# Gating the side matmuls of a one-layer hybrid decoder to every fourth step, moving delta-net arithmetic from GpSimd to VectorE, and spreading the small inverse products

## The chip, the cores and the metric

The kernel runs on one core of a Trainium2 chip. A core has five engines with instruction queues of their own: TensorE (PE, the matmuls; its weight loads are listed as PEld), VectorE (DVE), ScalarE (ACT), GpSimd (POOL) and SyncE (SP, which here issues all the DMAs). Matmul results land in PSUM, everything else lies in SBUF. The metric is the device time of one execution in microseconds (us), the median of several runs; lower is better.

## The reference, cut to what matters

One decoder layer with `D_MODEL` 2048 over 16 learned meta tokens and 256 real tokens (272 positions in all), float32:

```
u = rmsnorm(h, attn_norm_w); proj = u @ w_in          # 2048 x 7184
o_a = diff_attention(aq, ak, av, ...)                 # 8 heads, two softmax maps a head
o_d = gated_deltanet(dq, dk, dv, dz, db, da, ...)     # 8 heads, chunked delta rule
h = h + concat([o_a, o_d]) @ w_out
u = rmsnorm(h, ffn_norm_w)
h = h + (silu(u @ w_gate) * (u @ w_up)) @ w_down      # hidden 5632
```

In the delta net q, k and v pass a causal convolution of four taps and SiLU, q and k are normalised, and each chunk needs the decay matrix `exp(gc_i - gc_j)` below the diagonal, the product `k k^T` scaled with it, the inverse of the unit lower triangular matrix `1 + L` made of it, and the state that goes from chunk to chunk:

```
decay = where(incl, exp(diff), 0)
lmat = where(strict, einsum(kb, kc) * decay, 0)
u, w = solve(1 + lmat, ...)
qk = einsum(qc, kc) * decay
v_new = u_c - w_c @ S;  o = (q_c * exp(g_c)) @ S + qk_c @ v_new
S = S * exp(g_last) + (k_c * exp(g_last - g_c))^T @ v_new
o = rmsnorm(o, o_norm_w) * silu(z)
```

## The kernel before, in words

**Main stream.** Every large product is made of three passes in a reduced float32 type: each weight tile `raw` (512 KB, loaded by SP into a ring of `WR` = 4) is split into `hi` (ACT copy, L250) and `lo` (DVE subtraction, L251), both in rings of `WS` = 4, and the activations are split in the same way. `proj` (L1086) multiplies 28 groups of 256 columns of `w_in`: first k, v, q and z of the delta net, then k, q and v of the attention, two heads at a time. A weight tile of `proj` carries 24 matmuls. `stream` (L1133) does the output projection, the gate, up and down projections.

**Side tasks.** Everything else is written as Python generators, run by `Tasks`. After each k-tile `proj` calls `tasks.step()` (six matmuls of the main stream per step), and `stream` calls it twice per k-tile. A step resumes up to `PER_STEP` = 2 tasks in list order. A task that yields a number sleeps that many steps, one that yields a condition sleeps until it holds. A `Ring` counts the live buffers of a pool: `aux` has four PSUM banks, and a task that wants to put side matmuls on TensorE takes one with `yield from aux.get(...)` and releases it with `aux.free()` once the reading instruction has been written down. `r1` (12 buffers) and `r2` (10) hold SBUF scratch. The four PSUM banks of `mm` belong to the main stream.

**What sets the order.** `manual_schedule` pins ACT and SP to the order in which the code writes their instructions. The instructions of PE, DVE and POOL are put into queues by the framework's planner: program order is the priority, but an instruction which the planner holds to be not ready is overtaken. [...]

**The delta net.** `decay` makes the decay matrix of a unit (four heads of one 128-position block): POOL multiplies a mask with the gate column (L475), four side matmuls (L479), an exponential on ACT, and POOL applies the triangle (L485). There are four units and the meta block. `unit` then multiplies that by `c1` on POOL (L792), forms `k k^T` (L795), multiplies both on DVE (L798), and waits for the inverse. `inverses` writes the 128x128 matrices to DRAM and back in 16x16 pieces, inverts these in 15 steps on DVE (L630, L631), returns them through DRAM, and doubles the size twice with many small products: L663 (a group of 32x32 pieces), a copy to SBUF, L677, a subtraction, with sleeps of two, one and two steps between them. POOL makes its masked operand at L624. After the inverse `unit` runs a chain of PSUM groups (L808, L819, L828, L836, L844, L851, L861); its `ks` is scaled by POOL at L815. `meta_block` has POOL scale eight `ksm` slices (L759). `z_task` applies SiLU on ACT and the output norm weight on POOL (L911); the gated result is formed at L888.

**Start.** SP issues `aw`, then pieces of `xT` with weight tiles 0 to 3 between them, then `w_ba`, `cmask` and `par`. The loop over k-tiles splits the input into `xh` and `xl` (L325, L326) and splits weight tile 0 in two halves after k = 0, and tiles 1, 2, 3 whole after k = 5, 9 and 13.

## Time and profile before

| what | value |
|---|---|
| time, median of 3 runs | 1263.71 us (1262.24 to 1264.34) |
| the profiled execution | 1262.79 us |
| its span, first to last instruction | 1261.0 us |
| mean granted TensorE clock | 0.996 |
| DMA, mean over the span | 178 GB/s |

The profiled execution took 1.8 us more than its span; that is what lies around the first and last instruction. The page lists busy time by engine, the span in slices, the chain of work that ended last, and groups of instructions by source line. A matmul in float32 is recorded as two instructions. In a timeline a bracket such as `[3.07 <-DVE gT L735]` gives the idle time of the engine just before the row, and the instruction that ended it. In a windows table each row is a stretch of the span: busy us and number of instructions of PE, PEld, DVE, ACT and POOL, then the granted clock as a share of full speed, the DMA share and GB/s. In the chain each row has a start, a length in us, and what the time was spent on.

### The profile page before, as it was taken

Reading aid. Unit: us, or ns where it says so; the run is one execution under the profiler, and the core shown is the slowest. Engines: PE = TensorE matmul, PEld = TensorE weight load, DVE = VectorE, ACT = ScalarE, POOL = GpSimd, SP = SyncE. Lnnn points to the kernel's source line nnn. Section 1 sums busy time; section 2 is a strip of 40 time slices with the busy share of each in tenths; the row PEclk is TensorE's granted clock in tenths of the full one; section 3 lists DMA queues with packets and bytes.
Section 4 is the critical chain, followed back from the end, with each engine's and each line's share of the span. In section 5 each row is a group of like instructions: output and inputs, shape, how many; then the busy total and the mean of one; then the engine's idle time right before and its main releaser. Section 6 shows DMA issues by size and latency. Waiting matters only on the chain.

```text
span 1261.0 us, 18878 instructions
## 1 busy us (share of the span) xinstructions
PE 1244.4 (99%) x7469; PEld 1092.2 (87%) x7469; DVE 729.4 (58%) x1084; ACT 610.9 (48%) x962; POOL 46.8 (4%) x48
## 2 busy tenths in 40 slices
PE   8999999999999999999999999999999999999998
PEld 7998989999999988888888888888888888888886
DVE  7789956567676666645544554554455454544443
ACT  6664454466776655544344444444444433343332
POOL 0322200110000000000000000000000000000000
PEclk9999999999999999999999999999999999999999
DMA  8456642345544655566665566556666555656562
GB/s 270 134 168 176 179 138 85 118 151 167 158 144 151 218 167 183 177 194 191 190 190 190 187 192 192 184 186 198 185 189 194 187 191 190 215 189 213 191 210 83
DMA packets 150280, 224.31 MB, mean 178 GB/s; under 512 B 11560, under 2 KB 72368, under 8 KB 149936
## 3 DMA queue, kind: packets, MB, share of 16 engines
q1 hardware_dynamic: 150192, 223.11, 55.8%
q8 instruction: 58, 0.95, 0.3%
q14 instruction: 30, 0.25, 0.1%
HBM read 219.73 MB, written 3.35 MB: 177 GB/s over the span
## 4 chain that ended last, share of the span: by engine, by line
PE 89%; DVE 6%; ACT 2%; DMA 1%; issue 1%; SPq 0%; DVEq 0%; ACTq 0%
PE mm L1133 64%; PE mm L1086 19%; DVE lo L251 2%; DVE r L514 1%; DMA raw<-in_w_in_dram 1%; PE aux L1216 1%; PE aux L1034 1%; ACT hi L250 1%; PE aux L989 1%; DVE r L630 0%; PE aux L1021 0%; PE aux L381 0%; SPq L276 0%; DVE r L631 0%; DMA e<-r 0%
## 5 line engine op out<-in xcount | busy, mean ns | idle before, releaser
L251 DVE TENSOR_TENSOR lo<-raw,hi 128x1024 fp32r<-128x1024 f32 (+1 forms) x409 | 504.9, 1236 | 469.5 <-ACT hi L250 468.4
L250 ACT CAST hi<-raw 128x1024 fp32r<-128x1024 f32 (+1 forms) x409 | 428.8, 1050 | 546.7 <-PE mm L1133 447.7
L1133 PE MATMUL mm<-hi,uh 128*128 128x512 f32 x704 | 274.9, 390 | 0.0
L1133 PE MATMUL mm<-hi,ul 128*128 128x512 f32 x704 | 274.0, 389 | 0.0
L1133 PE MATMUL mm<-lo,uh 128*128 128x512 f32 x704 | 273.9, 389 | 0.0
L1086 PE MATMUL mm<-xh,hi 128*128 128x272 f32 (+2 forms) x896 | 260.7, 291 | 1.6 <-ACT hi L250 1.6
L1086 PE MATMUL mm<-xh,lo 128*128 128x272 f32 (+2 forms) x896 | 255.6, 286 | 3.0 <-issue 1.8
L1086 PE MATMUL mm<-xl,hi 128*128 128x272 f32 (+2 forms) x896 | 256.7, 287 | 0.0
L1133 PE MATMUL mm<-hi,hT 128*128 128x512 f32 x704 | 217.2, 389 | 0.0
L1086 PEld LDWEIGHTS mm<-xh,hi 128*128 128x128 f32 x896 | 169.6, 189 | 5.8 <-issue 3.0
L1086 PEld LDWEIGHTS mm<-xh,lo 128*128 128x128 f32 x896 | 168.8, 189 | 1.9 <-DVE lo L251 1.9
L1086 PEld LDWEIGHTS mm<-xl,hi 128*128 128x128 f32 x896 | 169.3, 189 | 0.3 <-DVE xl L326 0.2
L1133 PEld LDWEIGHTS mm<-hi,ul 128*128 128x128 f32 x704 | 132.1, 188 | 27.6
L1133 PEld LDWEIGHTS mm<-hi,hT 128*128 128x128 f32 x704 | 132.1, 188 | 27.3
L1133 PEld LDWEIGHTS mm<-hi,uh 128*128 128x128 f32 x704 | 132.2, 188 | 27.1
L1133 PEld LDWEIGHTS mm<-lo,uh 128*128 128x128 f32 x704 | 132.2, 188 | 27.0
L1133 PE MATMUL mm<-lo,hT 128*128 128x512 f32 x352 | 136.9, 389 | 0.0
L1133 PEld LDWEIGHTS mm<-lo,hT 128*128 128x128 f32 x352 | 66.1, 188 | 13.7
L514 DVE SCALAR_TENSOR_TENSOR r<-r,par_sb,r 128x272 f32<-128x272 f32 (+1 forms) x72 | 34.7, 541 | 0.2 <-ACT r L511 0.2
L1133 PE MATMUL mm<-hi,mix_d_hi 128*128 128x512 f32 x64 | 25.5, 399 | 0.0
L1133 PE MATMUL mm<-hi,mix_a_hi 128*128 128x512 f32 x64 | 25.1, 392 | 0.0
L1133 PE MATMUL mm<-hi,mix_d_lo 128*128 128x512 f32 x64 | 25.0, 390 | 0.0
(305 smaller groups left out, 849.8 us busy)
## 6 DMA issues: line engine op xcount, KB each, us to landing
raw<-in_w_in_dram SPq DMA_DIRECT2D x111, 512.0 KB, 3.6
raw<-in_w_gate_dram SPq DMA_DIRECT2D x88, 512.0 KB, 3.5
raw<-in_w_up_dram SPq DMA_DIRECT2D x88, 512.0 KB, 3.5
raw<-in_w_down_dram SPq DMA_DIRECT2D x88, 512.0 KB, 3.5
raw<-in_w_out_dram SPq DMA_DIRECT2D x32, 512.0 KB, 3.5
xr<-in_xT_dram SPq DMA_DIRECT2D x7, 272.0 KB, 6.0
x_k_c<-in_x_dram SPq DMA_DIRECT2D x1, 1024.0 KB, 6.5
x_q_c<-in_x_dram SPq DMA_DIRECT2D x1, 1024.0 KB
```

The lines of the kernel that those rows point to most:

```text
L250: S.copy(hi[:, js], raw[:, js])
L251: V.tensor_tensor(lo[:, js], raw[:, js], hi[:, js], ALU.subtract)
L514: V.scalar_tensor_tensor(acc, raw[:, off + j:off + j + m], cwv[:, ct, j:j + 1], acc, ALU.mult, ALU.add)
L989: PE.matmul(pss[m][:, cut[n]], q[ms, P * n:P * (n + 1)], k[ms, 0:NK[n]], start=True, stop=True)
L1034: PE.matmul(po[:, n, :], l, r, start=(j == 0), stop=(j == 1 + n))
L1086: PE.matmul(acc[c][:, 0:n], a[:, k, cs], b[:, kt, t0:T], start=(kt == 0 and i == 0), stop=(kt == KT - 1 and i == 2))
L1133: PE.matmul(acc[b], l, r[:, i % 2, :], start=(first and i == 0 and j == 0), stop=(last and i == len(kts) - 1 and j == 2))
L1216: PE.transpose(pst[:, j, :], g_[:, P * j:P * (j + 1)], ident)
```

## The change

There are four parts.

1. `aux.get` now also needs `tasks.slot()`, which holds in every fourth step (`SLOT` = 4). In such a step up to six tasks are resumed, in the others two as before. A side task that wants a PSUM bank therefore sleeps until the next slot; SBUF rings and the main stream's banks are not gated.
2. Delta-net arithmetic leaves POOL: the two products of `decay`, the masked operand of `inverses`, the `ksm` and `ks` scalings run on DVE. The multiplication by `c1` is no longer a step of its own but a factor in two DVE instructions, which become four instructions of 128x128 each. The output norm weight moves from POOL in `z_task` into the DVE instruction that forms the gated result.
3. The sleeps between the small inverse products become 5, 3 and 5 steps in place of 2, 1 and 2.
4. At the start weight tile 4 is loaded ahead of `w_ba`, `cmask` and `par`, and tiles 1 to 3 are split in halves, after k = 4, 8 and 12, each followed by the load of one more tile.

```diff
+SLOT = 4
 class Ring:
     def get(self, *shape):
-        while self.live >= self.bufs:
-            yield lambda: self.live < self.bufs
+        ok = lambda: self.live < self.bufs and self.slot()
+        while not ok():
+            yield ok
         return self.now(shape or None)
...
+    def slot(self):
+
+        return self.t % SLOT == 0
     def step(self):
         self.t += 1
-        left = self.per_step
+        left = 3 * self.per_step if self.slot() else self.per_step
...
-    aux = Ring(auxp, "aux", 4, 512)
+    aux = Ring(auxp, "aux", 4, 512, tasks.slot)
...
-    nc.sync.dma_start(out=wba_raw, in_=w_ba)
-    nc.sync.dma_start(out=cmsk, in_=cmask)
-    nc.sync.dma_start(out=par_sb, in_=par)
...
         if k == 0:
             split_to(1, 2)
-        elif k in (5, 9, 13):
-            split_to((k + 3) // 4)
+            load_to(5)
+            for dst, src in ((wba_raw, w_ba), (cmsk, cmask), (par_sb, par)):
+                nc.sync.dma_start(out=dst, in_=src)
+        elif k in (4, 8, 12):
+            split_to(k // 4 + 1, 2)
+            load_to(k // 4 + 5)
...
# decay
-        G.tensor_tensor(gt, bc_mid(mk("tri_s"), m), bc_last(gcols, P), ALU.mult)
+        for h in range(m):
+            V.tensor_scalar(gt[:, h, :], mk("tri_s"), gcols[:, h:h + 1], None, ALU.mult)
...
-        G.tensor_tensor(dst, dst, bc_mid(tri, m), ALU.mult)
+        V.tensor_tensor(dst, dst, bc_mid(tri, m), ALU.mult)
...
# inverses
-        G.tensor_tensor(gm[:, f, :], gT[:, f, :], bc_mid(mk("off16"), 8), ALU.mult)
+        V.tensor_tensor(gm[:, f, :], gT[:, f, :], bc_mid(mk("off16"), 8), ALU.mult)
...
-            yield 2
+            yield 5
...
-            yield 1
+            yield 3
...
-                yield 2
+                yield 5
...
# meta_block
-                G.tensor_scalar(t[:, h, :], ktm["m"], c2m[:, 4 * g + h:4 * g + h + 1], None, ALU.mult)
+                V.tensor_scalar(t[:, h, :], ktm["m"], c2m[:, 4 * g + h:4 * g + h + 1], None, ALU.mult)
...
# unit
-        G.tensor_tensor(dq, dq, bc_last(c1[:, cs], P), ALU.mult)
...
-        yield 3
-        yield 1
-        V.tensor_tensor(dt, ps, dq, ALU.mult)
+        yield 4
+        for i in range(4):
+            V.scalar_tensor_tensor(dt[:, i, :], ps[:, i, :], c1[:, cs][:, i:i + 1], dq[:, i, :], ALU.mult, ALU.mult)
...
-            G.tensor_tensor(ks, ks, bc_last(c2[:, cs], P), ALU.mult)
+            for i in range(4):
+                V.tensor_scalar(ks[:, i, :], ks[:, i, :], c2[:, cs][:, i:i + 1], None, ALU.mult)
...
-        V.tensor_tensor(dq, ps, dq, ALU.mult)
+        for i in range(4):
+            V.scalar_tensor_tensor(dq[:, i, :], ps[:, i, :], c1[:, cs][:, i:i + 1], dq[:, i, :], ALU.mult, ALU.mult)
...
-        V.tensor_tensor(val, ps, sz[:, 4 * g:4 * g + 4, P * n:P * (n + 1)], ALU.mult)
+        V.scalar_tensor_tensor(val, ps, pr("onorm"), sz[:, 4 * g:4 * g + 4, P * n:P * (n + 1)], ALU.mult, ALU.mult)
...
# z_task
-        act(z, z, AF.Silu)
-        yield 1
-        G.tensor_scalar(sz[:, h, :], z, pr("onorm"), None, ALU.mult)
+        act(sz[:, h, :], z, AF.Silu)
```

## The prediction

> **What bounds the kernel now.** I read the page first, then the chain of work that ended last, by engine.

> ```profile
> span 1261.0 us, 18878 instructions
> ...
> PE 1244.4 (99%) x7469; PEld 1092.2 (87%) x7469; DVE 729.4 (58%) x1084; ACT 610.9 (48%) x962; POOL 46.8 (4%) x48
> ...
> PE 89%; DVE 6%; ACT 2%; DMA 1%; issue 1%; SPq 0%; DVEq 0%; ACTq 0%
> ```

> TensorE is the bound: it is idle for only 1261.0 − 1244.4 = 16.6 us. The change removes no matmul, so it can gain in two ways: a side matmul costs less beside others of its kind, or TensorE waits less. For the second I went through TensorE's timeline and took every row with a wait that the change could touch.

> ```profile
> 21.59 0.39 PE L1086 MATMUL mm<-xh,hi 128*128 128x272 f32 x1 [0.70 <-ACT hi L250]
> ...
> 54.53 0.44 PE L539 MATMUL aux<-cmsk,k_c 128*128 128x128 f32 x2 [1.72 <-ACT k_c L196]
> ...
> 98.37 2.05 PE L795 MATMUL aux<-k_c 128*128 128x128 f32 x8 [3.07 <-DVE gT L735]
> ...
> 166.19 0.38 PE L1086 MATMUL mm<-xh,lo 128*128 128x260 f32 x1 [1.80 <-issue]
> ...
> 274.10 0.63 PE L884 MATMUL aux<-cmsk,r 128*128 128x128 f32 x4 [0.47 <-DVE small L309]
> ```

> Together 7.8 us of waiting; I call the rows S (start), A, B, C and D. All lie in the first 275 us, where the delta net runs; what the wait costs beyond itself comes below.

> **Grouping the side matmuls.** The merged chain gives the price of a group by its size; two neighbours in TensorE's timeline show the change of kind.

> ```profile
> 315.90 1.09 PE aux L1021 x10
> ...
> 320.61 2.23 PE aux L1034 x20
> ...
> 337.95 9.02 PE mm L1086 x72
> ...
> 574.30 0.87 PE aux L1216 x8
> 575.17 43.54 PE mm L1133 x192
> ```

> ```profile
> 619.34 0.47 PE L1133 MATMUL mm<-hi,uh 128*128 128x512 f32 x1
> 619.65 0.39 PE L1133 MATMUL mm<-lo,uh 128*128 128x512 f32 x1
> ```

> Eight records take 0.87 us, ten 1.09, twenty 2.23: 0.109, 0.109 and 0.112 each, with no fixed part that a larger group would share. The first main matmul after a group does take longer (0.31 us from start to start, against 43.54 / 192 = 0.227), but the group's own price per record does not show it as a loss. I take **nothing** for grouping. The upper bound: if that 0.08 us were saved at each of some 40 groups (an estimate: in the delta net and the attention about half of the groups would join another), 3 us. It cannot well cost anything by itself, as the same records run.

> What the gate does cost is delay: up to three steps at each bank. I looked for a consumer that it could reach. The last two attention heads, counted in steps from the end of `proj`: five gated banks (slots 4, 8, 20, 24, 32) and the write at step 35; `stream` reaches their k-tiles after 16 k-tiles of the delta-net half and six of the attention half, at step 44. So nine steps are left over. The delta net has far more room:

> ```profile
> 244.41 1.78 PE aux L861 x16
> ...
> 430.43 1.37 PE mm L1133 x6
> ```

> Its last chain product ends at 246.2 and its first consumer, the output projection, starts at 430.4. In the other direction the delay helps: an instruction that reads a bank has up to four steps before another task takes the bank.

> **POOL's work on DVE.** This carries most of the forecast. The timelines of POOL and DVE side by side:

> ```profile
> 46.49 5.38 POOL L475 TENSOR_TENSOR r<-cmsk,ga 128x128 f32<-128x128 f32 x5 [46.06 <-DVE ga L449]
> ...
> 89.43 4.36 POOL L792 TENSOR_TENSOR qkT<-qkT,c 128x512 f32<-128x512 f32 x4 [10.76 <-DVE c L573]
> 93.75 2.43 POOL L815 TENSOR_TENSOR r<-r,c 128x512 f32<-128x512 f32 x2
> 99.50 2.37 POOL L624 TENSOR_TENSOR gm<-gT,cmsk 128x1024 f32<-128x1024 f32 x1 [3.32 <-DVE gT L798]
> ```

> ```profile
> 50.89 3.54 DVE L514 SCALAR_TENSOR_TENSOR r<-r,par_sb,r 128x272 f32<-128x272 f32 x6
> ...
> 74.82 2.56 DVE L514 SCALAR_TENSOR_TENSOR r<-r,par_sb,r 128x272 f32<-128x272 f32 x6
> ...
> 91.60 4.88 DVE L514 SCALAR_TENSOR_TENSOR r<-r,par_sb,r 128x272 f32<-128x272 f32 x4
> ...
> 100.08 2.88 DVE L251 TENSOR_TENSOR lo<-raw,hi 128x1024 fp32r<-128x1024 f32 x1
> ...
> 111.77 1.22 DVE L251 TENSOR_TENSOR lo<-raw,hi 128x1024 fp32r<-128x1024 f32 x1
> ```

> Six convolution steps take 2.56 us when POOL is idle (0.43 each); beside POOL's products four take 4.88 (1.22 each), and at 50.89, partly beside L475, six take 3.54. A `lo` takes 2.88 instead of 1.22. So in these rows alone POOL's tensor_tensor costs DVE 3.2 + 1.0 + 1.7 = 5.9 us. This is what makes A and B: DVE is late against the planned order, and TensorE stands at a bank that DVE has yet to read (B), or at a `k_c` whose convolution is late (A).

> B costs more than its 3.07 us. Its eight records take 2.05 and not 0.87, and the main matmuls behind it run slow too:

> ```profile
> 98.37 2.05 PE aux L795 x8
> 100.42 5.55 PE mm L1086 x41
> ```

> 41 matmuls at 9.02 / 72 = 0.125 are 5.14 us, so B is 3.07 + 1.18 + 0.41 = **4.7 us**. With POOL's products gone and banks held longer, I take 4.4 of it back, and for A its 1.7.

> Now what moves. The DVE prices, by groups:

> ```profile
> L822 DVE SCALAR_TENSOR_TENSOR r<-aux,ne_gc,r 128x128 f32<-128x128 f32 x16 | 4.4, 343 | 0.5 <-PE aux L819 0.5
> ...
> L798 DVE TENSOR_TENSOR gT<-aux,qkT 128x512 f32<-128x512 f32 x4 | 2.6, 676 | 0.0
> ...
> L753 DVE TENSOR_SCALAR r<-aux,ksq 128x128 f32<-128x128 f32 x1 | 0.3, 336 | 0.0
> ...
> L746 DVE TENSOR_SCALAR c2m<-par_sb,c 128x8 f32<-128x8 f32 x1 | 0.2, 216 | 0.0
> ```

> No row shows a tensor_scalar of 128x128 out of SBUF at rest; between 0.216 (8 columns) and 0.336 (128 columns out of PSUM) I take 0.28. 17 for L475, 8 for L759 and 8 for L815 make 33 × 0.28 = 9.2 us (7.1 to 11.1). Four triangles of 128x512 at 0.676 are 2.7 (and 0.3 for the meta block), two masked operands at a `lo`'s 1.22 are 2.4. Two products of each of four units become 4 × 0.343 in place of 0.676: 8 × 0.70 = 5.6. Sum 20.2 us, less the 5.9 given back: at most 14 us more on DVE, spread from 46 to some 290 us. What hides it is that `lo` is written ahead; where DVE is full this cover is thinnest:

> ```profile
> 88.00:99.00 11.00, 7.93 (x64) 7.74 (x64) 11.00 (x15) 4.40 (x7) 6.75 (x6) 0.94 0.25 77
> ...
> 110.00:150.00 40.00, 40.00 (x329) 40.00 (x328) 39.45 (x110) 20.14 (x28) 2.49 (x3) 1.00 0.63 189
> ```

> From 110 to 150 DVE is busy 39.45 of 40 us and TensorE still never idles. Into 88 to 150 move 2.8 (first `c1` factor), 2.2 (L815), 2.4 (L624) and 2.2 (L759) = 9.6, and 3.2 + 1.7 = 4.9 come back. Net 4.7 us, against a ring of four `lo` tiles of 24 × 0.125 = 3.0 us each: up to 12 us of cover. I take no cost, and keep the other end for a rival. L911's removal frees POOL alone; it had no waiter on TensorE.

> **Spreading the inverse products.** The chain around C, and one microsecond of the windows:

> ```profile
> 161.44 0.73 PE aux L677 x54
> ...
> 163.30 0.66 PE aux L663 x54
> ...
> 164.39 1.80 issue
> 166.19 2.33 PE mm L1086 x10
> 168.52 1.39 PE aux L772 x8
> ```

> ```profile
> 166.00:167.00 1.00, 0.81 (x4) 0.81 (x4) 0.00 (x0) 0.00 (x0) 0.00 (x0) 0.51 0.10 33
> ```

> After two bursts of tiny matmuls within 2.6 us TensorE stops for 1.80 us with no releaser, and then runs at half the granted clock: ten main matmuls take 2.33 instead of at most 1.25, eight records 1.39 instead of 0.87. C is 1.80 + 1.08 + 0.52 = 3.4 us. With eight steps between L663 and L677 of the same inverse the bursts lie some 6 us apart (8 × 6 × 0.125). I read "issue" after a burst as instructions arriving too slowly, and take back **2.7**; the rest stays for a chance that both inverses meet in one slot. [...]

> **Start and the rest.** In S TensorE waits 0.70 us for `hi` of tile 4, whose load now goes ahead of three others: 0.7. For D, one more step or two before L884: 0.4.

> **The sum.** 1.7 + 4.4 + 2.7 + 0.7 + 0.4 = 9.9 us. Against it I set one new wait of A's size, 1.8, as up to six tasks now meet in one step and ask for four banks. In C 1.80 us of idle was followed by half clock, in A 1.72 was not, so its price is 1.8 to 3.4. [...] The profiled execution, 1261.0 + 1.8 around it = 1262.8, becomes 1262.8 − 8.1 = 1254.7; the median of the runs lies 0.9 above that execution, so **1255.6**.

> **The rivals.** Changes below 0.2%, 2.5 us, can't be told from none here.

> - *The inverse products still stop TensorE.* For it: both inverses may fall into the same slot, and no row proves the cause. Against: the stop came only after the second burst in a row. Then C stays: 1255.6 + 2.7 = 1258.3. Chance 0.2.
> - *No new wait, everything returned, and grouping saves something.* 1255.6 − 1.8 − 1.5 (half of its bound) = 1252.3. For it: from 285 to 430 us, without POOL, no wait of this size occurs. Chance 0.15.
> - *The waits only move.* The gate brings readers and takers of banks into the same steps, and A and B come back as waits for other banks: 1.7 + 4.4 are not gained, 1255.6 + 6.1 = 1261.7, within 0.2%. Chance 0.12.
> - *DVE becomes the bound from 88 to 150 us.* Net 4.7 us more on an engine with 0.5 to spare: if `lo` runs less than about 4 us ahead there, TensorE waits 4.2 us, loses 1.6 to half clock as in C, and A to D go on in another form: 1263.7 + 5.8 = 1269.5. Against: TensorE was at full rate there. Chance 0.13.

> The forecast itself has 0.4. Faster: 0.4 + 0.2 + 0.15 = 0.75; same 0.12; slower 0.13. The range from 1250 (the second rival, with 2 us for the unknown size of the moved instructions) to 1264 (the third) leaves out the last rival and a little below.

> **What would show it.** After the change L514 should take 0.43 each throughout 45 to 110 us, with no `lo` above 1.3; the rows of A and B should have no wait above 0.5; the windows from 88 to 110 should show full clock. L663 and L677 should lie apart with no "issue" after them. Twenty records of L1034 should still take 2.2 us. A wait of L1086 for `lo` L251 after 80 us would make me wrong, and so would banks waiting for the new four-part products.

## The result, and the profile after

| kernel | median, us | runs |
|---|---|---|
| before | 1263.90 | 4 (1262.24 to 1264.34) |
| after | 1251.94 | 4 (1251.06 to 1253.56) |

The ratio is 0.9909, with a 95% interval from 0.9892 to 0.9926: 12.0 us faster. The forecast was 1255.6, the range 1250 to 1264. The profiled execution after took 1252.28 us.

The page of the changed kernel, its span, the engines and the chain by engine:

```profile
span 1250.5 us, 18895 instructions
...
PE 1241.4 (99%) x7469; PEld 1090.6 (87%) x7469; DVE 731.9 (59%) x1151; ACT 609.6 (49%) x965; POOL 6.1 (0%) x14
...
PE 93%; DVE 3%; ACT 2%; DMA 1%; issue 1%; SPq 0%; DVEq 0%; ACTq 0%
```

TensorE is idle for 1250.5 − 1241.4 = 9.1 us, 7.5 less than before, and busy for 3.0 us less with the same records: slow stretches behind the waits went too. POOL's 46.8 us fell to 6.1, and DVE has only 2.5 us more than before. TensorE's waits in the same kernel (whom it waited for, us in total, times, the longest):

```profile
PE aux L276 <- DVE r L510: 1.2, 1, 1.2
PE mm L1094 <- ACT hi L257: 1.2, 2, 0.8
PE mm L1094 <- DVE lo L258: 0.8, 1, 0.8
PE aux L953 <- ACT r L1033: 0.6, 3, 0.2
...
PE aux L894 <- DVE r L890: 0.3, 1, 0.3
```

The lines of the code moved by 7 to 10: L250 is now L257, L251 L258, L514 L523, L539 L548, L663 L672, L677 L686, L795 L803, L884 L894, L1086 L1094. The rows A (L539), B (L795) and C ("issue") are not there any more. D's wait for `small` (0.47) is gone too; L894 waits 0.3 for `r`, where L884 waited 0.2. The three largest all lie in the first 23 us.

Where the time came from, read off both timelines: every pair of input projections has 96 main matmuls, and the table has the start of the first one of some pairs (the first pair is 0, and starts at 6.2 us before and 6.1 after).

| pair | before, us | after, us | difference |
|---|---|---|---|
| 1 | 21.6 | 20.8 | −0.8 |
| 2 | 40.4 | 40.9 | +0.5 |
| 3 | 60.5 | 58.9 | −1.6 |
| 5 | 85.6 | 83.8 | −1.8 |
| 6 | 105.9 | 99.7 | −6.2 |
| 10 | 153.0 | 146.9 | −6.1 |
| output projection | 430.3 | 420.7 | −9.6 |

In these two executions, then, the start (S) lost 0.5, A gave 2.1, B 4.4, C and D together 3.5, and 0.9 came after 430 us (10.5 in all, by rounding). The windows of the changed kernel (us of the window, busy us and instructions of PE, PEld, DVE, ACT and POOL, then granted clock, DMA share, GB/s):

```profile
88.00:99.00 11.00, 11.00 (x93) 11.00 (x92) 8.21 (x28) 4.99 (x11) 0.00 (x0) 1.00 0.55 167
110.00:150.00 40.00, 40.00 (x330) 40.00 (x329) 38.68 (x116) 18.43 (x25) 2.09 (x3) 1.00 0.58 171
```

TensorE was busy 7.93 of 11 us in the first of these windows before; now it is full, at full clock, and DVE has room. From 110 to 150 DVE is as full as before, and TensorE never idles.

The chain of the changed kernel answers the question of group prices (start, length, records):

```profile
93.37 2.68 PE aux L803 x24
...
99.07 0.89 PE aux L803 x8
```

Three units' products now stand in one group: 24 records at 0.112 us, eight at 0.111. A larger group is no cheaper per record here; the twenty records of L1034, now L1042, took 2.38 us.

### The profile page after: what moved, and what is told of

The parts are those of the page before. It is cut to its first block, busy times and chain, and to the rows that moved or that the text cites. A ratio compares the mean times of both kernels' runs of the same rounds, so it can differ in the third digit from the quotient of the medians.

```text
span 1250.5 us, 18895 instructions
## 1 busy us (share of the span) xinstructions
PE 1241.4 (99%) x7469; PEld 1090.6 (87%) x7469; DVE 731.9 (59%) x1151; ACT 609.6 (49%) x965; POOL 6.1 (0%) x14
## 4 chain that ended last, share of the span: by engine, by line
PE 93%; DVE 3%; ACT 2%; DMA 1%; issue 1%; SPq 0%; DVEq 0%; ACTq 0%
PE mm L1141 64%; PE mm L1094 22%; DVE lo L258 1%; PE aux L1224 1%; PE aux L1042 1%; DMA raw<-in_w_in_dram 1%; PE aux L997 1%; ACT hi L257 0%; PE aux L548 0%; SPq L283 0%; PE aux L871 0%; PE aux L828 0%; PE aux L803 0%; PE aux L853 0%; PE aux L845 0%
## 5 line engine op out<-in xcount | busy, mean ns | idle before, releaser
L258 DVE TENSOR_TENSOR lo<-raw,hi 128x1024 fp32r<-128x1024 f32 (+1 forms) x412 | 499.3, 1214 | 453.5 <-ACT hi L257 453.0
L257 ACT CAST hi<-raw 128x1024 fp32r<-128x1024 f32 (+1 forms) x412 | 429.0, 1044 | 561.2 <-PE mm L1141 448.8
L1094 PE MATMUL mm<-xh,hi 128*128 128x272 f32 (+2 forms) x896 | 258.9, 290 | 1.2 <-ACT hi L257 1.2
L1094 PE MATMUL mm<-xl,hi 128*128 128x272 f32 (+2 forms) x896 | 256.3, 286 | 0.3 <-DVE xl L330 0.3
L1094 PE MATMUL mm<-xh,lo 128*128 128x272 f32 (+2 forms) x896 | 255.7, 286 | 0.8 <-DVE lo L258 0.8
L1094 PEld LDWEIGHTS mm<-xh,hi 128*128 128x128 f32 x896 | 169.3, 189 | 3.1 <-ACT hi L257 1.6
L1094 PEld LDWEIGHTS mm<-xh,lo 128*128 128x128 f32 x896 | 169.0, 189 | 1.2 <-DVE lo L258 1.2
L1094 PEld LDWEIGHTS mm<-xl,hi 128*128 128x128 f32 x896 | 169.3, 189 | 0.6 <-DVE xl L330 0.5
L523 DVE SCALAR_TENSOR_TENSOR r<-r,par_sb,r 128x272 f32<-128x272 f32 (+1 forms) x72 | 30.9, 488 | 0.6 <-ACT r L520 0.5
L1141 PE MATMUL mm<-lo,mix_d_hi 128*128 128x512 f32 x64 | 25.0, 390 | 0.0
```

Source lines behind the costliest of these rows:

```text
L257: S.copy(hi[:, js], raw[:, js])
L258: V.tensor_tensor(lo[:, js], raw[:, js], hi[:, js], ALU.subtract)
L523: V.scalar_tensor_tensor(acc, raw[:, off + j:off + j + m], cwv[:, ct, j:j + 1], acc, ALU.mult, ALU.add)
L1094: PE.matmul(acc[c][:, 0:n], a[:, k, cs], b[:, kt, t0:T], start=(kt == 0 and i == 0), stop=(kt == KT - 1 and i == 2))
L1141: PE.matmul(acc[b], l, r[:, i % 2, :], start=(first and i == 0 and j == 0), stop=(last and i == len(kts) - 1 and j == 2))
```

## The experiments

The change was cut into its four parts: **pool** (2 of the list above), **slot** (1), **spread** (3) and **start** (4). "only" adds one part to the kernel before; "no" takes one from the kernel after. The runs came in three batches, each with its own runs of the kernel before. Most medians are of four runs; only_spread has five, only_start ten, burst3 two.

| run | median, us | ratio to before, 95% interval |
|---|---|---|
| only_pool | 1257.59 | 0.9945 [0.9926, 0.9963] |
| no_pool | 1252.56 | 0.9906 [0.9884, 0.9928] |
| only_slot | 1256.35 | 0.9937 [0.9918, 0.9956] |
| no_slot | 1254.97 | 0.9921 [0.9897, 0.9945] |
| only_spread | 1259.27 | 0.9965 [0.9952, 0.9978] |
| no_spread | 1255.81 | 0.9942 [0.9921, 0.9964] |
| burst3 | 1277.74 | 1.0110 [1.0082, 1.0139] |
| only_start | 1263.82 | 0.9999 [0.9989, 1.0009] |
| no_start | 1251.92 | 0.9904 [0.9889, 0.9919] |
| after_again | 1252.02 | 0.9904 [0.9889, 0.9919] |
| late_rms | 1251.09 | 0.9895 [0.9879, 0.9912] |
| lean | 1252.94 | 0.9911 [0.9896, 0.9925] |

The kernel before had 1263.38 in the first batch (the first four rows), 1264.17 in the second (only_spread, no_spread, burst3, only_start), 1264.02 in the third.

### A and B: POOL's products, or the gate

```diff
# only_pool: before, with part 2 of the change, in its core
-        G.tensor_tensor(gt, bc_mid(mk("tri_s"), m), bc_last(gcols, P), ALU.mult)
+        for h in range(m):
+            V.tensor_scalar(gt[:, h, :], mk("tri_s"), gcols[:, h:h + 1], None, ALU.mult)
...
# only_slot: before, with part 1
+        ok = lambda: self.live < self.bufs and self.slot()
...
+        left = 3 * self.per_step if self.slot() else self.per_step
...
# no_pool and no_slot: after, with the same lines taken back
```

Expected of only_pool:

> The kernel before with the delta-net arithmetic moved from POOL to DVE and nothing else. Theory 1 (POOL's tensor_tensor slows DVE, and that makes waits A and B): both waits gone, no L514 group above 0.5 us each, C still there: 1263.9 - 6 = about 1258. Rival (the waits come from banks that are taken again too soon, so the gate cures them): A and B remain as waits of TensorE for DVE or ACT, time within 0.2% of before, 1261.5 to 1266.

Expected of no_pool:

> The changed kernel with POOL's share of the delta net put back; gate, spread sleeps and start as changed. Theory 1: DVE is again slowed beside POOL's products (L514 at about 1.2 us each), and TensorE waits 3 to 6 us in all between 45 and 110 us: 1256 to 1258. Rival: the gate alone covers DVE's delay, the time stays at 1252 to 1253.

Expected of only_slot:

> The kernel before with the gate alone (side matmuls begin in every fourth step, six tasks there). Theory 1: DVE remains slow beside POOL; B shrinks by at most half, because the bank is taken up to three steps (2.3 us) later, A stays: 1259 to 1263. Rival: A and B gone, about 1258. If merging groups saved time by itself, the price per record of L1034 (20 records, 2.23 us) would fall; both expect it not to.

Expected of no_slot:

> The changed kernel without the gate: two tasks a step, banks taken in any step; the rest as changed. Theory 1: A and B stay away, 1252 to 1254; D (wait of L884 for its rescaled output) and the wait of L1054 in the output projection return, some 1 us. Rival: waits of TensorE for DVE come back, 1256 or more.

Pool alone gave 5.8 us, slot alone 7.0. The time and the waits of only_pool came as expected, but C went as well, to 0.26 us. In no_pool and only_slot the rival came true: the gate alone removes A and B. no_slot lies above its 1252 to 1254, with 0.4 us of D back and no wait of L1054. Taken from the change, pool is missed by nothing that can be measured, and slot by less than the runs of no_slot differ among themselves (1251.54 to 1256.67). Either part alone removes both waits: from 45 to 130 us only_pool and no_slot have no row of TensorE's waits at all, only_slot and no_pool one of 0.3 us. The two parts remove the same waits, so their gains don't add: the four parts alone gave 5.8 + 7.0 + 4.9 + 0.4 = 18.1 us, the change 12.0. The 6.1 us in between (each of the sums is uncertain by some 2 us) are about what A and B were worth, 6.1 in the prediction and 6.5 in the table above. That fits, but the sums hold more than A and B (only_pool lost C and got another wait there, see below).

In no_pool DVE is still held up. Its timeline, POOL and DVE:

```profile
100.88 2.40 POOL L632 TENSOR_TENSOR gm<-gT,cmsk 128x1024 f32<-128x1024 f32 x1
101.16 3.21 DVE L258 TENSOR_TENSOR lo<-raw,hi 128x1024 fp32r<-128x1024 f32 x1
...
104.29 4.70 DVE L522 SCALAR_TENSOR_TENSOR r<-r,par_sb,r 128x272 f32<-128x272 f32 x6
104.51 2.54 POOL L632 TENSOR_TENSOR gm<-gT,cmsk 128x1024 f32<-128x1024 f32 x1
```

One `lo` takes 3.21 us, six convolution steps 4.70 instead of 2.56, and TensorE does not wait. So a late DVE was a necessary half of A and B, not their whole cause. The other half was the time at which TensorE meets the banks: with the gate the next task can't take a bank as soon as it is given up. This second half is argued from the rule of the gate; the runs show that the gate removes the waits, not by which bank.

These rows also suggest what the slowing is. POOL's instruction ends at 100.88 + 2.40 = 103.28, and the `lo` ends 1.09 us later, about its own length (1.15 at 109.20 in the same timeline). In the kernel before, the `lo` of 2.88 us at 100.08 ends 1.08 us after L624. So in these rows it looks as if the `lo` did not run slower, but worked only when POOL was done. In the same kernel the four steps of 1.22 us each stand beside POOL instructions of 1.09 (L792, four in 4.36) and 1.22 (L815, two in 2.43): one POOL instruction per DVE instruction, and each of the four steps ends 0.3 us after a POOL instruction does.

### C: the inverse products

```diff
# only_spread: before, with part 3; no_spread: after, with it taken back
-            yield 2
+            yield 5
...
-            yield 1
+            yield 3
...
-                yield 2
+                yield 5
...
# burst3: after, with every product of L672 and L686 issued three times
-            for h in range(8):
+            for h in list(range(8)) * 3:
```

Expected of only_spread:

> The kernel before with the longer sleeps between the small inverse products alone. Theory 1 (C comes from two bursts of tiny matmuls close together): the 1.80 us of issue and the half clock after it are gone, A and B stay: 1263.4 - 3.4 = about 1260. Rival: C stays or moves, 1262 to 1265.

Expected of no_spread:

> The changed kernel with the old sleeps of 2, 1 and 2 between the small inverse products. Theory 1: without the spread the bursts follow every four steps (3 us), and an issue wait of 1 to 2 us returns near 155 to 175 us, with half clock: 1253.5 to 1256. Rival: the gate alone spreads enough, 1252.

Expected of burst3:

> The changed kernel with each small inverse product issued three times into the same place: bursts of 192 recorded matmuls and as many weight loads in place of 64. By their own price that is 2 x (0.84 us a burst) x 8 bursts = 13 us more, some 1265. Theory (a burst outruns the arrival of instructions, which the page lists as packets of queue q8): beyond that price TensorE shows issue waits of 1 to 2 us behind several bursts, and half clock after them: 1270 to 1280. Rival (C was no question of the number of instructions): the price alone, no issue wait above 0.5 us behind the bursts.

The spread alone gave 4.9 us, and without it the change loses 0.33% (from 0.9909 to 0.9942; each is uncertain by some 0.2%). The 4.9 is more than the 3.4 that C was worth, but its interval reaches from 2.8 to 6.1. In only_spread A and B stand as before and C is gone: from 150 to 205 us TensorE has one wait of 0.7 us, at L763 for DVE. Its waits from 45 to 130 us:

```profile
PE aux L795 <- DVE gT L735: 3.0, 1, 3.0
PE aux L539 <- ACT k_c L196: 1.7, 1, 1.7
```

The chain of no_spread shows what the short sleeps do under the gate. (A chain counts only the records that it runs through. Tiny records run beside each other: 64 of 0.18 us each take 0.73 us in the timeline, and x54, x52 or x35 in a chain are such 64.)

```profile
156.49 1.04 ACT hi L257
157.53 0.17 ACT r L677
...
157.75 0.69 PE aux L686 x52
158.44 0.65 PE aux L672 x35
159.09 0.64 issue
159.73 0.66 PE aux L548 x4
```

Two things happen. TensorE waits (1.65 us in the timeline) for the copy L677, which stands behind a `hi` of 1.04 us on ACT; and both inverses' bursts then fall into one group, as the prediction feared, after which TensorE stops for 0.64 us. The four runs of no_spread fall into two pairs, 1254.0 and 1254.1 us at a mean clock of 1.000 and 0.999, and 1257.5 and 1258.0 at 0.996; this trace is of the first pair and has no half clock here. only_pool has the same wait, 2.47 us, behind the same copy, half clock for 6.8 us after it, and a stop of only 0.26. So two things can go wrong at this place, a copy that comes late on ACT and a stop behind bursts, and longer sleeps remove both. The same place has both in only_slot, 0.87 us for the copy and 1.09 us of "issue" in TensorE's timeline. In the changed kernel the bursts of both inverses follow each other at 3 to 5 us, and the chain has no stop:

```profile
156.80 0.73 PE aux L672 x54
157.53 0.59 PE aux L548 x4
158.12 2.89 PE mm L1094 x24
161.01 0.22 PE aux L772 x2
161.23 0.66 PE aux L686 x54
```

burst3 brings the stop back. It has 768 records more than the changed kernel, not the 1024 of the expectation, as some bursts have 32 records and not 64. Rows of TensorE's timeline:

```profile
157.07 1.26 PE L672 MATMUL aux<-r,gm 32*32 32x16 f32 x128 [0.19 <-DVE r L651]
161.17 1.05 PE L672 MATMUL aux<-r,gm 32*32 32x16 f32 x64 [2.84 <-issue]
168.12 1.54 PE L686 MATMUL aux<-r,r 32*32 32x16 f32 x162
171.66 0.43 PE L686 MATMUL aux<-r,r 32*32 32x16 f32 x30 [2.00 <-issue]
179.25 1.56 PE L686 MATMUL aux<-r,r 32*32 32x16 f32 x165
183.54 0.42 PE L686 MATMUL aux<-r,r 32*32 32x16 f32 x27 [2.73 <-issue]
```

After 128, 162 and 165 of 192 tiny records TensorE stops for 2.84, 2.00 and 2.73 us with no releaser, in the middle of one burst; this kernel differs from the changed one in the number of these records alone. Another 1.81 us comes at 204.69 after 188 records. The first burst of 192, at 151.91, has no stop, and neither have two of 96 records that take longer each (1.71 us for 96, against 1.26 for 128 above; at 189.38 and 194.07). Together that is 9.4 us of stops. The rest of the 23.2 us by which its span is longer is the added records and a low clock behind three of the stops.

In these runs not the length of a burst decided where the stop fell, but a place in TensorE's stream of instructions. Counted from 0 over all its records in order of their start (in before 14938 matmuls and weight loads and 62 semaphore and drain records), the first record after each stop of burst3 is number 3009, 3522, 4033 and 5058. The stops of before, no_spread, only_slot, only_pool and of only_start (2.31 us) all end at 2753 or 2754. All these lie whole multiples of 256 apart, within one. And each of the nine ends 1.2 to 1.5 us after a packet of 16 KB of the queue q8, which the page calls "instruction", has landed (in before the packet at 164.90, the stop's end at 166.19); burst3 has 64 of these packets and the changed kernel 58, six more for 1536 more matmuls and weight loads, or 256 a packet. By this TensorE waited for its instructions; it is read from the packets, as no row names a releaser. The spans between these places give the price: the 256 records up to a stop took 1.3 to 2.9 us (5.0 in only_pool, whose stop is the shortest), and no other span of 256 took less than 4.4 us. The changed kernel's shortest is 4.6 us, so it is not far from a stop.

### S: the start

```diff
# only_start: before, with part 4; no_start: after, with it taken back
...
# late_rms: after, with
-    tasks.spawn(input_rms(), delay=0)
+    tasks.spawn(input_rms(), delay=5)
...
# lean: before, with parts 1 and 3 and delay=5, nothing else
```

Expected of only_start:

> The kernel before with the new order of loads and the split halves at the start alone. By my term S: tile 4 ready 0.7 us earlier, about 1262.7, nothing else changed. Rival: at the start DVE and ACT, not the load, set when tile 4 is split, so the time stays at 1263.4; A, B and C as before in both.

Expected of no_start:

> The changed kernel with the loads and splits at the start as before. Theory (the start part gives nothing, since the first split that TensorE waits for, the hi of the fifth piece of weights, stands on ACT behind four squares of input_rms, which the change does not move): within 1.5 us of the changed kernel in this batch, 1251 to 1254 us, with the wait for hi at about 21 us still 0.7 us. Rival (the start part gives its 0.7 us or more and its loss in the first profile was chance): 1.5 to 3 us slower than the changed kernel.

Expected of after_again:

> The changed kernel as it is, on the same chip as the three runs beside it, as their yardstick. Both theories: ratio to the kernel before 0.991 (0.989 to 0.993), about 1252 to 1253 us, with waits of L1094 of 0.77 us for hi L257 and 0.76 us for lo L258 between 20 and 23 us, as in its first profile.

Expected of late_rms:

> The changed kernel with input_rms begun 5 steps later, so that on ACT the hi of the fifth piece comes ahead of the four squares (2.29 us at 17.52 in the profile of the changed kernel). Theory (the squares are what the start waits for): the waits of L1094 for hi (0.77 us) and lo (0.76 us) at 20 to 23 us go, no half clock follows them (22 to 26 us: 0.63 and 0.52 in the profile of the changed kernel, worth 1.7 us there and less in others), so 1.5 to 3 us faster than the changed kernel in this batch, 1249.5 to 1251 us. Rival (rbc comes 5 steps later, and the first convolution frees its bank later, so a wait of TensorE at 40 us takes the place): 0 to 1 us slower than the changed kernel, and a wait for r L510 above the 1.2 us that stand there now.

Expected of lean:

> The kernel before with three small edits only: the gate of four steps, the longer sleeps of the inverse, and input_rms begun 5 steps later; POOL's products and the loads at the start stay as before. Theory (gate or POOL part cures the waits at 54 and 98 us alone, the sleeps the stop at 166 us, and the squares set the start): as fast as late_rms within 1.5 us, 1249.5 to 1252.5 us, with POOL's products still slowing single DVE rows (an lo above 2 us near 56 or 101 us) and TensorE not waiting there. Rival (the POOL part is needed beside the spread): 3 us or more slower than late_rms, 1253 to 1256 us, with a wait over 0.7 us between 50 and 200 us.

The start part gives nothing that the medians show: 0.9999 alone, and no_start equals the change to 0.1 us. In the kernel before it was the load that came last. The tile landed at 20.40 us, after the four squares of `input_rms` (L340), and ACT had been idle for 0.76 us; the name in the bracket is not the releaser that counts:

```profile
17.45 2.28 ACT L340 ACTIVATE r<-xr 128x544 f32<-128x544 f32 x4
20.50 1.05 ACT L250 CAST hi<-raw 128x1024 fp32r<-128x1024 f32 x1 [0.76 <-DVE lt L426]
```

In after_again the tile landed at 17.68. Its timeline, ACT and TensorE:

```profile
17.80 2.28 ACT L348 ACTIVATE r<-xr 128x544 f32<-128x544 f32 x4
19.99 1.03 ACT L257 CAST hi<-raw 128x1024 fp32r<-128x1024 f32 x1
...
21.07 0.39 PE L1094 MATMUL mm<-xh,hi 128*128 128x272 f32 x1 [0.81 <-ACT hi L257]
22.59 0.51 PE L1094 MATMUL mm<-xh,lo 128*128 128x272 f32 x2 [0.75 <-DVE lo L258]
```

The `hi` that TensorE waits for now stands on ACT right behind the four squares; an earlier load can help it no further. It begins 0.5 us earlier than before (0.8 in the profile of the change), but TensorE gets there earlier too, as two waits at 10.9 and 12.1 us shrank from 0.95 and 0.50 to one of 0.25, and so it waits as long as before. In late_rms the squares come after it:

```profile
18.25 1.04 ACT L257 CAST hi<-raw 128x1024 fp32r<-128x1024 f32 x1
19.19 2.30 ACT L348 ACTIVATE r<-xr 128x544 f32<-128x544 f32 x4
22.89 1.05 ACT L257 CAST hi<-raw 128x1024 fp32r<-128x1024 f32 x1 [1.41 <-DVE r L351]
...
23.99 0.39 PE L1094 MATMUL mm<-xh,hi 128*128 128x272 f32 x1 [0.29 <-ACT hi L257]
25.25 0.52 PE L1094 MATMUL mm<-xh,lo 128*128 128x272 f32 x2 [0.50 <-DVE lo L258]
```

Both waits go, and two smaller ones come a tile later, where ACT was idle for 1.41 us before the next `hi`. The row names DVE, but the load of that tile landed at 22.79, 0.1 us ahead of `hi`, so the load came last. The gain is 0.9 us (1252.02 to 1251.09), where 1.5 to 3 were expected. In lean, without the early load, the same edit leaves S as it was: TensorE waits 0.70 us at 21.5. ACT's timeline:

```profile
20.41 1.05 ACT L257 CAST hi<-raw 128x1024 fp32r<-128x1024 f32 x1 [2.94 <-DMA raw<-in_w_in_dram]
21.37 2.30 ACT L347 ACTIVATE r<-xr 128x544 f32<-128x544 f32 x4
```

The tile landed at 20.31 there. So S has two bounds, the squares on ACT and the load, one right behind the other. The start part moves one, late_rms the other, and only both together remove the wait.

lean took 1252.94 us, 11.1 less than before in its batch, with three small edits and POOL's work where it was. It is 1.85 us behind late_rms, between the two theories; 1.0 of that is there at the first matmul of pair 1 (21.5 against 20.5 us). But the first main matmul of all is 1.2 us later in lean's profile (6.8 against 5.6), and after_again, with the same start as late_rms up to there, has 6.8 too; so what of the 1.85 belongs to S is open, and the rest was not followed. late_rms has the lowest median of all, and its interval overlaps with that of the change.

## Why the prediction was right, and where it was not

- **Bound.** TensorE's waits and the low clock behind them were the gain, as forecast; grouping gave nothing, as forecast. The rival that let grouping save 1.5 us has the time nearest to the result (1252.3), but not for that reason.
- **A and B.** Sized well: 1.7 + 4.4 forecast, 2.1 + 4.4 found. The reason was half of it. The prediction gave both to POOL's products and let the gate help beside; the runs show that the gate alone removes them too, with DVE still held up. Its measures, no `lo` above 1.3 us and full clock from 88 to 110, came true in the change, but a slow `lo` alone, 3.21 us in no_pool, did not make TensorE wait.
- **C and D.** 2.7 + 0.4 forecast, 3.5 found. "Instructions arriving too slowly" stood the test of burst3 and of the places of the stops. What the prediction missed is that the stop fell at a place in the stream (the places lie multiples of 256 records apart) and not behind any second burst, and that a copy behind a `hi` on ACT can take its place, with a wait of 1.65 us in no_spread and 2.47 in only_pool.
- **S.** This step failed: 0.7 forecast, nothing found. The prediction rightly took the load for what `hi` waited for, but credited its whole wait to the load and did not look at what stood ahead of that `hi` on ACT. The squares, in the timeline of before at 17.45 for 2.28 us, are the next bound, and TensorE waited 0.77 us again.
- **The new wait.** 1.8 us were set aside for tasks meeting in a slot. The largest new wait is L953 for ACT, 0.6 us in three pieces; two more of 0.2 are at L488 and L672. That the 1.8 did not come is the largest part of the 2.4 us by which the profiled time undercut the sum (1252.28 against 1254.7); S and the loss at the start go the other way. So the sum holds errors of both signs, and its nearness to the result is in part luck.
- **DVE.** At most 14 us more were forecast, and 2.5 came. By the groups of both kernels the moved work costs 16.9 us and not 20.2, and more came back than the 5.9: 11.9, of it 5.5 in `lo`, 3.8 in the convolution and 2.6 in three small rows (rows of different groups overlap, so these sums don't give the 2.5 exactly). The groups of DVE in the changed kernel (busy us, mean ns of one, idle us before):

```profile
L806 DVE SCALAR_TENSOR_TENSOR gT<-aux,c,qkT 128x128 f32<-128x128 f32 x16 | 4.4, 342 | 0.0
L484 DVE TENSOR_SCALAR r<-cmsk,ga 128x128 f32<-128x128 f32 x17 | 3.4, 280 | 0.0
L768 DVE TENSOR_SCALAR r<-ktm_m,c2m 128x128 f32<-128x128 f32 x8 | 1.8, 275 | 0.0
```

The durations of one were right (0.28 and 0.343 forecast). But instructions in a row overlap: 17 take 3.4 us, 0.20 each and not 0.28, and 16 take 4.4, 0.275 and not 0.343. The row of L822 that the prediction quoted already said so: x16, 4.4. Here busy time by count is the price in a sum, and the mean of one a latency. So L475's 17, for one, cost 3.4 us and not 4.8, and the rival in which DVE becomes the bound had less under it than it seemed.

- **Inverse products, waits that move.** The rival that C stays came true only without the spread. The one that A and B come back as other waits has no row for it.

## What to carry to other kernels

Before summing the gains of several edits, ask of each wait how many of the edits would cure it alone: parts that cure the same wait don't add, and the cheapest of them does. When a wait names a releaser, read what stood ahead of the releaser on its own engine, and what stood ahead of that, before crediting an edit with the wait. Price moved work by busy time over count, not by the mean duration of one instruction (0.20 against 0.28 us here). Where tiny matmuls come in bursts, look at how long each 256 records of TensorE last: in these runs spans of 2.9 us or less had stops of 0.6 to 2.8 us, and spans of 4.4 or more had none but one of 0.26.

## What the runs showed of the hardware

- **Tiny records outran their instructions in these runs.** The nine stops, of 0.26 to 2.84 us, end at records of TensorE that lie whole multiples of 256 apart, within one (2753 in before, 3009 to 5058 in burst3), 1.2 to 1.5 us after a 16 KB packet of the instruction queue has landed. That the next instructions came with that packet was not shown; it is read from the places and from the count of packets, 256 records a packet.
- **The same waits, another clock.** The profile of the changed kernel has the two waits at 20 to 23 us as after_again has them, within 0.05 us. In the windows behind them the first kernel's execution was granted this:

```profile
22.00:24.00 2.00, 1.68 (x8) 1.68 (x9) 2.00 (x6) 2.00 (x4) 0.00 (x0) 0.63 0.91 269
24.00:26.00 2.00, 2.00 (x11) 2.00 (x11) 2.00 (x3) 1.13 (x2) 0.00 (x0) 0.52 0.65 218
```

and after_again this:

```profile
22.00:24.00 2.00, 1.41 (x11) 1.41 (x12) 2.00 (x5) 1.93 (x4) 0.00 (x0) 1.00 0.89 267
24.00:26.00 2.00, 1.86 (x15) 1.65 (x14) 2.00 (x5) 1.70 (x3) 0.00 (x0) 1.00 0.82 254
```
